# A hybrid encoder block on one core: eleven units of the output projection read their moving columns from 2, 4, 8 or 16 pieces

## The chip, the cores and the metric

The kernel runs on one core of a Trainium2 chip. The metric is the device time of one execution in microseconds (us). Two runs of the kernel before gave 907.03 and 907.22 us, median 907.12 us. The profiled execution took 907.02 us, of which the span from its first to its last instruction is 905.3 us. PE is TensorE's matmul side, PEld its loading of the stationary operand, DVE is VectorE, ACT is ScalarE, POOL is GpSimd, SP is the engine that issues most of the loads.

## The reference, cut to what matters

One encoder block over 256 tokens of width 2048, all in float32. What touches the change is the output projection, which multiplies the 2048 concatenated group outputs of each token by a 2048 x 2048 matrix:

```python
h = _rmsnorm(x, norm1_g)
proj = h @ w_in
...
a = _rmsnorm(_window_attention(q, k, v, sink), attn_out_g)
f = _rmsnorm(_fourier_mix(u, w_fourier), fourier_out_g)
x = x + jnp.concatenate([a, f], axis=-1) @ w_out
x = x + _conv_ffn(_rmsnorm(x, norm2_g), w_up, dw_w, dw_b, w_down)
return _rmsnorm(x, normf_g)
```

## The kernel before, in words

Weights stream through the core in units of 128 x 2048 float32 (1 MB). For each unit, `load` (line 172) has SP fetch it into a buffer `raw` (three buffers), and `split` (line 179) makes two float32r tiles of it: ACT copies it, rounded, into `hi` (line 185), and DVE writes the rest, `raw - hi`, into `lo` (line 186). Both lie in one tile `parts` (three buffers) of 4224 elements a partition. `parts_tile` (line 167) sets where: for a unit of kind "moving", as the output projection's are, `hi` starts at element 0 and `lo` at element 2048. A product of two float32 matrices then takes three float32r matmuls: hi x hi, lo x hi, hi x lo.

The work runs in a written order, one unit after another: `unit` (line 415) does the unit's matmuls, and `step` (line 395) then splits the unit two places ahead. Units 0 to 3 of the plan belong to the Fourier input, 4 to 7 to the values, 8 to 23 to keys and queries (`N_OUT` is 24), 24 to 39 to the output projection, and the rest to the feed-forward part. Other work (attention steps, sums, transposes) is hung before, beside or behind a unit by `at`.

A unit of the output projection (the loop from line 831 on) holds the weights of one block of 512 output columns `c` and one quarter `kq` of the 2048 inputs: four tiles q of 128 inputs x 512 columns. `OUT_ORDER` (line 54) lists (c, kq). For each of the two halves b of the tokens, `moving_weights` (line 365) runs over the four tiles. The stationary operand is a 128 x 128 block of `cat` (inputs x tokens) and the moving operand is the tile of weights, in three matmuls (lines 370 to 372) of 512 columns each:

```python
for q, k in enumerate(kk, q0):
    ah, al = (block(act(k), part, b, halves) for part in range(2))
    wh, wl = (in_turn(w[:, q * n : (q + 1) * n]) for w in (hi, lo))
    nc.tensor.matmul(ps, ah, wh, start=first and q == q0, stop=False)
    nc.tensor.matmul(ps, al, wh, start=False, stop=False)
    nc.tensor.matmul(
        ps, ah, wl, start=False, stop=last and q == q0 + len(kk) - 1
    )
```

So a unit is 2 x 4 x 3 = 24 matmuls of 512 columns. The results are accumulated in PSUM in `ps_a` (attention inputs, kq 0 to 2) or `ps_ff` (Fourier inputs, kq 3).

The moving columns of a tile are not read one after another. `in_turn` (line 130) reads the 512 elements of a tile from two pieces of 256, one element of the first, one of the second, and so on; the pieces lie 256 elements (1 KB) apart. The host has permuted the weights so that the columns come out in their order. Every float32r matmul of this kernel reads its moving operand from two pieces 1 KB apart: `from_halves` (line 136) does it for attention, `still_weights` (line 376, lines 387 and 389) for the matmuls whose stationary operand is the weights.

Of the kernel before, what the change touches and what calls it, by code (L numbers as in the profile page):

```python
# [9 lines left out]
F32R = mybir.dt.float32r  # L10
# [3 lines left out]
P = 128  # L14
# [37 lines left out]
N_OUT = N_QK + len(QK_ORDER)  # L52

OUT_ORDER = [(0, 0), (1, 0), (0, 1), (1, 1), (0, 3), (0, 2), (1, 3), (1, 2)]
OUT_ORDER += [(c, k) for c in (2, 3) for k in range(4)]


GROUPS = [list(range(4))] + [list(range(k, k + 8)) for k in range(4, 36, 8)]
# [38 lines left out]
def block_kernel(  # L97
# [22 lines left out]
    wp = ctx.enter_context(tc.tile_pool(name="wp", bufs=1))  # L120
# [9 lines left out]
    def in_turn(ap):  # L130
        return ap.rearrange("p (a e) -> p e a", a=2)
# [30 lines left out]
    raws, halves = {}, {}  # L162
# [4 lines left out]
    def parts_tile(name, place):  # L167
        t = wp.tile([P, 2 * 2048 + 128], F32R, tag="parts", name=name, bufs=3)
        oh, ol = PLACES[place]
        return t[:, oh : oh + 2048], t[:, 2048 + ol : 4096 + ol]  # L170
# [8 lines left out]
    def split(i):  # L179
        if i >= len(units):  # L180
            return
        _, n, place = units[i]
        raw = raws[i][:, 0:n]
        hi, lo = (t[:, 0:n] for t in parts_tile(f"parts{i}", place))
        nc.scalar.activation(hi, raw, AF.Copy)  # L185
        nc.vector.tensor_tensor(lo, raw, f32(hi), ALU.subtract)  # L186
        halves[i] = hi, lo
        load(i + RAW)
        load_more(i + RAW)
# [32 lines left out]
    ps = bank(dn, "ps_warm")  # L222
# [19 lines left out]
    for c in range(4):  # L242
        t = base.tile([P, 4, 512], F32R, tag=f"hT{c}", name=f"hT{c}")
# [42 lines left out]
    k = 0  # L286
# [75 lines left out]
        nc.vector.tensor_copy(by_parity(dst), ps.rearrange("p (a e) -> p a e", a=2))  # L362


    def moving_weights(hi, lo, n, kk, act, b, ps, first, last, q0=0, halves=False):

        for q, k in enumerate(kk, q0):
            ah, al = (block(act(k), part, b, halves) for part in range(2))
            wh, wl = (in_turn(w[:, q * n : (q + 1) * n]) for w in (hi, lo))
            nc.tensor.matmul(ps, ah, wh, start=first and q == q0, stop=False)  # L370
            nc.tensor.matmul(ps, al, wh, start=False, stop=False)  # L371
            nc.tensor.matmul(  # L372
                ps, ah, wl, start=False, stop=last and q == q0 + len(kk) - 1
            )
# [456 lines left out]
    for n, (c, kq) in enumerate(OUT_ORDER):  # L831
        i = N_OUT + n

        def work(hi, lo):
            if kq == 0:
                ps_a[c] = [bank(mm, f"ps_a{c}{b}") for b in range(2)]
            if kq == 3:
                ps_a[c, "f"] = [bank(dn, f"ps_ff{c}{b}") for b in range(2)]
            ps = ps_a[c] if kq < 3 else ps_a[c, "f"]
            for b in range(2):  # L840
                moving_weights(
                    hi, lo, 512, range(4 * kq, 4 * kq + 4), cat.get, b, ps[b],
                    kq in (0, 3), kq in (2, 3),
                )

        unit(i, work)
        if kq >= 2:
            part = "a" if kq == 2 else "f"
            ps = ps_a[c] if kq < 3 else ps_a[c, "f"]
            last = c in added  # L850
            added.add(c)
            if n == len(OUT_ORDER) - 1:
                later.append(out_post(c, part, ps))
                continue

            at(behind if (c, kq) == (0, 2) else beside, i + 1, out_add, c, part, ps)
            if last:
                at(behind, i + 1, out_sums, c)
                at(before, i + 2, lambda c=c: st.update({("x", c): turn_x_in(c)}))
                at(beside, i + 2, lambda c=c: turn_x_out(c, st.pop(("x", c))))  # L860
# [7 lines left out]
    parts = {}  # L868
    gate_out, sums_of, act = {}, {}, {}
# [288 lines left out]
    for q in range(2):  # L1158
        kind, j = items[q]
        ps = bank(mm, f"ps_{kind}{j}")  # L1160
# [16 lines left out]
    for n, it in enumerate(items):  # L1177
# [8 lines left out]
        if it[0] in ("gate", "val"):  # L1186
            kind, j = it
            ps = bank(mm, f"ps_{kind}{j}")
# [4 lines left out]
        if it[0] == "product":  # L1193
            kind, g, c, p = it
            hi, lo = halves.pop(it)
            both = c == 2
            shape = (2, 1024) if both else (4, 512)
            for cc in (0, 1) if both else (c,):
                o = 512 * cc if both else 0
                if (cc, p) in held:  # L1200
                    first, end = (g, c) == FIRST_SET[cc], (g, c) == LAST_SET[cc]
                    by_parts(held[cc, p], parts[p], hi, lo, first, end, *shape, o)
                    continue
                ps = bank(mm, f"ps_{p}{g}{cc}")
# [6 lines left out]
        else:  # L1211
            kind, g, c = it
            hi, lo = halves.pop(up_index[n])
            ps = [bank(mm, f"ps_l{g}{c}{b}") for b in range(2)]
# [10 lines left out]
    i = up_index[n]  # L1225
# [49 lines left out]
def _layout(inp):  # L1275

    import numpy as np

    f = lambda a: np.ascontiguousarray(np.asarray(a), dtype=np.float32)
    x = f(inp["x"]).reshape(P, 2, D)  # L1280
    by_parity = np.arange(S).reshape(P, 2).T.reshape(-1)

    def in_turn(w):

        return f(w).reshape(*w.shape[:-1], -1, 256, 2).swapaxes(-1, -2).reshape(w.shape)

    def tiles(v):
        return f(v).reshape(-1, P).T

    def moving(w, cols):  # L1290

        return in_turn(w[:, cols]).reshape(-1, 4, P, cols.stop - cols.start).transpose(
            0, 2, 1, 3
        ).reshape(-1, P, 4 * (cols.stop - cols.start))

    def still(w, c0):

        return f(w[:, c0 : c0 + P]).reshape(-1, P, P).transpose(1, 0, 2).reshape(1, P, -1)

    w_in = np.asarray(inp["w_in"])  # L1300
    start = {"q": 0, "k": AW}
    kv = NKV * HD
    win = np.concatenate(
        [moving(w_in, slice(AW + kv, AW + 2 * kv))]
        + [still(w_in, start[t] + h * HD) for t, h in QK_ORDER]
    )
    u0 = AW + 2 * kv
    u_rows = np.concatenate(
        [x.transpose(1, 0, 2).reshape(S, NK, P).transpose(2, 1, 0),
         in_turn(w_in[:, u0 : u0 + FW]).reshape(NK, P, FW).transpose(1, 0, 2)], axis=2,  # L1310
    )
    w_out = np.asarray(inp["w_out"])
    wout = np.concatenate(
        [moving(w_out, slice(c * 512, (c + 1) * 512))[k : k + 1] for c, k in OUT_ORDER]
    )
    w_up = np.asarray(inp["w_up"])
    wup = np.concatenate(
        [still(w_up, o + j * P) for j in range(NF) for o in (0, DFF)]
    )
    w_dn = np.asarray(inp["w_down"])  # L1320
    def rows_by(tiles, cols, width=512):

        w = in_turn(w_dn[tiles[0] * P : (tiles[-1] + 1) * P, cols : cols + width])
        return w.reshape(len(tiles), P, width).transpose(1, 0, 2).reshape(P, -1)

    downs = []
    for g, c in SETS:
        half = len(GROUPS[g]) // 2
        width = 1024 if c == 2 else 512
        for k in (GROUPS[g][0], GROUPS[g][half]):  # L1330
            for n in (0, 1024):
                downs.append(rows_by(range(k, k + half), n + (0 if c == 2 else 512 * c), width))
    late = [rows_by(LATE, 512 * c) for c in range(4)]
    dw = f(inp["dw_w"]).reshape(3, NF, P).transpose(2, 1, 0).reshape(P, 3 * NF)
    sink = np.broadcast_to(f(inp["sink"])[None, :], (P, NH))
    vecs = np.concatenate(
        [tiles(inp["norm1_g"]), tiles(inp["norm2_g"]), tiles(inp["attn_out_g"]),
         tiles(inp["fourier_out_g"]), dw, tiles(inp["dw_b"]), sink], axis=1,
    )
    t = np.arange(S)  # L1340
    ang = 2.0 * np.pi * ((t[:, None] * t[None, :]) % S) / S
    c_pos = np.concatenate(
        [np.cos(ang[:, : S // 2 + 1]), np.sin(ang[:, 1 : S // 2])], axis=1
    )
    c_pos = c_pos[by_parity].reshape(2, P, P, 2).transpose(1, 3, 0, 2)
    k = np.arange(P)
    ang = 2.0 * np.pi * ((k[:, None] * k[None, :]) % P) / P
    c_chan = np.concatenate([np.cos(ang), -np.sin(ang)], axis=1) / np.sqrt(S * P)
    dist = np.abs(t[:, None] - t[None, :]).astype(np.float64)
    c_rel = np.where(dist <= WINDOW, dist, FAR)[by_parity][:, by_parity]  # L1350
    c_rel = c_rel.reshape(2, P, S).transpose(1, 0, 2)
    return {
        "x": x,
        "u_in": np.concatenate([tiles(inp["norm1_g"]), u_rows.reshape(P, -1)], axis=1),
        "vecs": np.ascontiguousarray(vecs),
        "wf": in_turn(f(inp["w_fourier"]).transpose(1, 0, 2).reshape(P, FW)),
        "w_in": win,
        "w_out": wout,
        "w_up": wup,
        "w_down": np.stack(downs),  # L1360
        "w_down_late": np.stack(late),
        "w_down_last": np.stack([rows_by(LAST, 512 * c) for c in range(4)]),
        "normf_g": f(inp["normf_g"]),
        "c_pos": np.ascontiguousarray(c_pos.reshape(P, 2 * S), dtype=np.float32),
        "c_chan": np.ascontiguousarray(c_chan, dtype=np.float32),
        "c_rel": np.ascontiguousarray(c_rel.reshape(P, 2 * S), dtype=np.float32),
    }
# [16 lines left out]
```

## Time and profile before

| | before |
|---|---|
| median of two runs | 907.12 us |
| profiled execution | 907.02 us |
| its span | 905.3 us |
| PE busy | 896.0 us (99%) |
| DVE busy | 746.2 us (82%) |
| ACT busy | 547.0 us (60%) |
| DMA moved | 214.86 MB, mean 237 GB/s |
| the output projection's matmuls | 384 of 512 columns, from 155.1 to 245.1 us |

A share of busy time is a mean over the span. Matmuls overlap in the pipeline: the profile's duration of one (380 ns for 512 columns) reaches from its start to its modelled end, and the next one starts before that. What a matmul costs in time is the distance from its start to the start of the next, which the timeline and the chain of work show. A group's row has its line, engine, operation and tiles, its shapes and count, then its busy time and mean ns of one, then the idle time of the engine before it and what ended that.

### The profile page before, as it was taken

What the parts mean: (1) busy time and instruction counts of PE and PEld (TensorE: products, weight loads), DVE (VectorE), ACT (ScalarE), POOL (GpSimd) and SP (SyncE); (2) the same over time, 40 slices, a digit from 0 to 9 for tenths busy, and PEclk for the clock granted to TensorE, in tenths of its full rate; (3) what the DMA queues carried; (4) which work ended last, traced back from release to release, by engine and by line L of the source; (5) the groups of instructions that cost most, each with busy time, mean ns of one, the idle gap of its engine ahead of it and who ended that gap; (6) DMA issues with size and microseconds to landing.
All of it is one profiled execution on the core that took longest, in us unless ns stands there. A gap on an engine that the chain in (4) does not pass through costs nothing.

```text
span 905.3 us, 12755 instructions
## 1 busy us (share of the span) xinstructions
PE 896.0 (99%) x5075; PEld 812.7 (90%) x5075; DVE 746.2 (82%) x893; ACT 547.0 (60%) x662; POOL 50.2 (6%) x64
## 2 busy tenths in 40 slices
PE   9999999999999999999999999999999999999996
PEld 8899999888899999999999999999999999999885
DVE  7579888666668877889887998878988789998996
ACT  7757677555554656556565565566655566656644
POOL 0001111000000000000000000000000000000003
PEclk9999999999999999999999999999999999999999
DMA  9864544456568677677898779887887988779652
GB/s 359 337 227 152 186 150 177 143 184 222 197 239 275 231 239 254 186 255 234 273 261 277 244 257 286 262 275 236 275 250 245 317 257 268 241 238 293 210 192 93
DMA packets 32764, 214.86 MB, mean 237 GB/s; under 512 B 3616, under 2 KB 3872, under 8 KB 8384
## 3 DMA queue, kind: packets, MB, share of 16 engines
q1 hardware_dynamic: 28592, 184.55, 54.5%
q0 software_dynamic: 4112, 29.49, 17.4%
q8 instruction: 40, 0.66, 0.3%
q14 instruction: 20, 0.16, 0.0%
HBM read 211.93 MB, written 2.10 MB: 236 GB/s over the span
## 4 chain that ended last, share of the span: by engine, by line
PE 95%; DVE 3%; POOL 1%; issue 1%; ACT 0%; ACTq 0%; POOLq 0%; DVEq 0%
PE ps_val L387 17%; PE ps_gate L387 17%; PE ps_val L389 8%; PE ps_gate L389 8%; PE ps_q L387 5%; PE ps_P L1098 3%; PE ps_P L1100 3%; PE ps_P L1099 3%; PE ps_N L1098 2%; PE ps_N L1099 2%; PE ps_N L1100 2%; PE ps_u L281 2%; PE ps_q L389 2%; PE ps_a L370 2%; PE ps_a L371 2%; PE ps_a L372 2%
## 5 line engine op out<-in xcount | busy, mean ns | idle before, releaser
L186 DVE TENSOR_TENSOR parts<-raw,parts 128x2048 fp32r<-128x2048 f32 (+1 forms) x129 | 293.2, 2273 | 48.7 <-ACT parts L185 47.9
L185 ACT ACTIVATE parts<-raw 128x2048 fp32r<-128x2048 f32 (+1 forms) x129 | 245.5, 1903 | 46.0 <-PE ps_a L372 12.4
L387 PE MATMUL ps_val<-hU,parts 128*128 128x512 f32 x688 | 227.7, 382 | 0.0
L387 PE MATMUL ps_gate<-hU,parts 128*128 128x512 f32 x688 | 227.3, 382 | 0.0
L389 PE MATMUL ps_val<-hU,parts 128*128 128x256 f32 x688 | 187.7, 273 | 0.0
L389 PE MATMUL ps_gate<-hU,parts 128*128 128x256 f32 x688 | 187.0, 273 | 0.0
L387 PEld LDWEIGHTS ps_val<-hU,parts 128*128 128x128 f32 x688 | 130.2, 189 | 18.0
L387 PEld LDWEIGHTS ps_gate<-hU,parts 128*128 128x128 f32 x688 | 130.1, 189 | 18.0
L389 PEld LDWEIGHTS ps_val<-hU,parts 128*128 128x128 f32 x688 | 132.3, 192 | 0.7
L389 PEld LDWEIGHTS ps_gate<-hU,parts 128*128 128x128 f32 x688 | 132.1, 192 | 0.9
L876 ACT ACTIVATE ft_g<-ps_gate 128x256 f32<-128x256 f32 x43 | 16.5, 383 | 112.6 <-PE ps_gate L389 110.0
L387 PE MATMUL ps_q<-hT,parts 128*128 128x512 f32 x192 | 62.6, 384 | 0.0
L876 ACT ACTIVATE ft_v<-ps_val 128x256 f32<-128x256 f32 x43 | 16.4, 382 | 73.4 <-PE ps_val L389 73.4
L1098 PE MATMUL ps_P<-parts_P,op_P 128*128 128x512 f32 x144 | 54.7, 380 | 0.0
L1100 PE MATMUL ps_P<-parts_P,op_P 128*128 128x512 f32 x144 | 54.7, 380 | 0.0
L1099 PE MATMUL ps_P<-parts_P,op_P 128*128 128x512 f32 x144 | 54.7, 380 | 0.0
L389 PE MATMUL ps_q<-hT,parts 128*128 128x256 f32 x192 | 50.4, 273 | 0.0
L984 DVE TENSOR_TENSOR parts_N<-sumw,parts_N 128x2048 fp32r<-128x2048 f32 x18 | 41.2, 2288 | 10.0 <-ACT parts_N L983 9.9
L1098 PE MATMUL ps_N<-parts_N,op_N 128*128 128x512 f32 x108 | 41.0, 380 | 0.0
L1100 PE MATMUL ps_N<-parts_N,op_N 128*128 128x512 f32 x108 | 41.0, 380 | 0.0
L1099 PE MATMUL ps_N<-parts_N,op_N 128*128 128x512 f32 x108 | 41.0, 380 | 0.0
L387 PEld LDWEIGHTS ps_q<-hT,parts 128*128 128x128 f32 x192 | 36.1, 189 | 4.6
(344 smaller groups left out, 1558.9 us busy)
## 6 DMA issues: line engine op xcount, KB each, us to landing
raw<-in_w_up SPq DMA_DIRECT2D x86, 1024.0 KB, 6.0
raw<-in_w_in SPq DMA_DIRECT2D x20, 1024.0 KB, 4.9
sumw<-in_w_down POOLq DMA_DIRECT2D x18, 1024.0 KB, 8.7
raw<-in_w_out SPq DMA_DIRECT2D x16, 1024.0 KB, 4.8
raw<-in_w_down_late SPq DMA_DIRECT2D x4, 1024.0 KB, 5.9
u_raw<-in_u_in SPq DMA_DIRECT2D x4, 768.0 KB, 10.8
raw<-in_w_down_last SPq DMA_DIRECT2D x4, 768.0 KB, 4.6
u_raw<-in_u_in SPq DMA_DIRECT2D x7, 384.0 KB, 6.5
```

The source lines that it names most:

```text
L185: nc.scalar.activation(hi, raw, AF.Copy)
L186: nc.vector.tensor_tensor(lo, raw, f32(hi), ALU.subtract)
L281: nc.tensor.matmul(ps_u[b], block(hk(k), part, b, True), in_turn(w), start=k == 0 and n == 0, stop=k == NK - 1 and n == 2,)
L370: nc.tensor.matmul(ps, ah, wh, start=first and q == q0, stop=False)
L371: nc.tensor.matmul(ps, al, wh, start=False, stop=False)
L387: nc.tensor.matmul(ps, hi[:, s], in_turn(h), start=k == 0, stop=False)
L389: nc.tensor.matmul(ps[:, 0:S], lo[:, s], in_turn(h)[:, 0:P], start=False, stop=k == NK - 1)
L876: nc.scalar.activation(tmp, ps[:, S : 2 * S], AF.Copy)
L984: nc.vector.tensor_tensor(lo, src, f32(hi), ALU.subtract)
L1098: nc.tensor.matmul(ps, o[:, 0, p, :], wh, start=first and p == 0, stop=False)
L1099: nc.tensor.matmul(ps, o[:, 1, p, :], wh, start=False, stop=False)
L1100: nc.tensor.matmul(ps, o[:, 0, p, :], wl, start=False, stop=end)
```

## The change

For eleven of the sixteen units of the output projection, numbers 1 to 7 and 9 to 12, the four tiles of 512 columns are laid out in another way in the unit's 2048 elements, and the matmuls read them in turn from another number of pieces at another distance. Units 0, 8, 13, 14 and 15 stay as they were. The table `READS` gives the number of pieces, their distance in elements of 4 bytes, the start of each of the four tiles, and a gap:

| unit | pieces | distance | elements a piece | c, kq |
|---|---|---|---|---|
| 1 | 4 | 512 B | 128 | 1, 0 |
| 2 | 2 | 2 KB | 256 | 0, 1 |
| 3 | 4 | 1 KB | 128 | 1, 1 |
| 4 | 8 | 1 KB | 64 | 0, 3 |
| 5 | 2 | 4 KB | 256 | 0, 2 |
| 6 | 8 | 256 B | 64 | 1, 3 |
| 7 | 4 | 2 KB | 128 | 1, 2 |
| 9 | 16 | 128 B | 32 | 2, 1 |
| 10 | 16 | 512 B | 32 | 2, 2 |
| 11 | 2 | 4 KB + 16 B | 256 | 2, 3 |
| 12 | 2 | 4 KB + 64 B | 256 | 3, 0 |

For units 11 and 12, `split` writes `hi` and `lo` in two rows of 1024 elements with the gap (4 or 16 elements) between them, so that the two pieces are 1028 or 1040 elements apart. `columns` builds the view that a matmul reads, and the host places the weights to match. The number of matmuls, their columns, their stationary operands, their order and the loads are the same.

```diff
+READS = {
+    1: (4, 128, [0, 512, 1024, 1536], 0),
+    2: (2, 512, [0, 256, 1024, 1280], 0),
+    3: (4, 256, [0, 128, 1024, 1152], 0),
+    4: (8, 256, [0, 64, 128, 192], 0),
+    5: (2, 1024, [0, 256, 512, 768], 0),
+    6: (8, 64, [0, 512, 1024, 1536], 0),
+    7: (4, 512, [0, 128, 256, 384], 0),
+    9: (16, 32, [0, 512, 1024, 1536], 0),
+    10: (16, 128, [0, 32, 64, 96], 0),
+    11: (2, 1024, [0, 256, 512, 768], 4),
+    12: (2, 1024, [0, 256, 512, 768], 16),
+}
...
         hi, lo = (t[:, 0:n] for t in parts_tile(f"parts{i}", place))
+        gap = READS.get(i - N_OUT, (0, 0, 0, 0))[3]
+        if gap:
+            t = wp.tile([P, 2 * 2048 + 128], F32R, tag="parts", name=f"parts{i}", bufs=3)
+            hi, lo = (
+                t[:, o : o + 2 * (1024 + gap)].rearrange("p (a e) -> p a e", a=2)[:, :, 0:1024]
+                for o in (0, 2 * (1024 + gap))
+            )
+            raw = raw.rearrange("p (a e) -> p a e", a=2)
         nc.scalar.activation(hi, raw, AF.Copy)
         nc.vector.tensor_tensor(lo, raw, f32(hi), ALU.subtract)
...
+    def columns(w, n, q, reads):
+        if reads is None:
+            return in_turn(w[:, q * n : (q + 1) * n])
+        pieces, far, places, gap = reads
+        o, m = places[q], n // pieces
+        if gap:
+            return w[:, :, o : o + m].rearrange("p a e -> p e a")
+        across = 2048 // (pieces * far)
+        w = w.rearrange("p (z a d) -> p z d a", z=across, a=pieces)
+        z, o = divmod(o, pieces * far)
+        return w[:, z, o : o + m, :]
+
-    def moving_weights(hi, lo, n, kk, act, b, ps, first, last, q0=0, halves=False):
+    def moving_weights(
+        hi, lo, n, kk, act, b, ps, first, last, q0=0, halves=False, reads=None
+    ):
 
         for q, k in enumerate(kk, q0):
             ah, al = (block(act(k), part, b, halves) for part in range(2))
-            wh, wl = (in_turn(w[:, q * n : (q + 1) * n]) for w in (hi, lo))
+            wh, wl = (columns(w, n, q, reads) for w in (hi, lo))
...
                 moving_weights(
                     hi, lo, 512, range(4 * kq, 4 * kq + 4), cat.get, b, ps[b],
-                    kq in (0, 3), kq in (2, 3),
+                    kq in (0, 3), kq in (2, 3), reads=READS.get(i - N_OUT),
                 )
```

The rest of the diff is on the host: `by_pieces` puts every `pieces`-th column of a tile into one piece.

More of the change, by code (lines that the diff above doesn't have):

```diff
@@ L1312, in _layout, with by_pieces @@
     w_out = np.asarray(inp["w_out"])
+    def by_pieces(n, w):
+        if n not in READS:
+            return in_turn(w).transpose(1, 0, 2).reshape(1, P, 2048)
+        pieces, far, places, _ = READS[n]
+        out = np.zeros((1, P, 2048), np.float32)
+        for o, tile in zip(places, w):
+            for a in range(pieces):
+                at = o + a * far
+                out[0, :, at : at + 512 // pieces] = tile[:, a::pieces]
+        return out
     wout = np.concatenate(
-        [moving(w_out, slice(c * 512, (c + 1) * 512))[k : k + 1] for c, k in OUT_ORDER]
+        [by_pieces(n, f(w_out[k * 512 : (k + 1) * 512, c * 512 : (c + 1) * 512]).reshape(
+            4, P, 512)) for n, (c, k) in enumerate(OUT_ORDER)]
     )
```

## The prediction

> **What bounds the kernel now.** I read the page first: busy shares, the 40 slices, the chain of work that ended last.
>
> ```profile
> span 905.3 us, 12755 instructions
> PE 896.0 (99%) x5075; PEld 812.7 (90%) x5075; DVE 746.2 (82%) x893; ACT 547.0 (60%) x662; POOL 50.2 (6%) x64
> ...
> PEclk9999999999999999999999999999999999999999
> ...
> PE 95%; DVE 3%; POOL 1%; issue 1%; ACT 0%; ACTq 0%; POOLq 0%; DVEq 0%
> ```
>
> PE is busy 99% of the span, its granted clock never drops, and 95% of the chain is PE. So the kernel is bound by TensorE as a whole. The change sits in one stage, so next come a window over that stage, its groups by line, and its waits.
>
> ```profile
> 155.10:245.10 90.00, 90.00 (x450) 1.00 0.54 187
> ```
>
> ```profile
> L370 PE MATMUL ps_a<-parts,cat 128*128 128x512 f32 x96 | 36.9, 384 | 0.0
> L186 DVE TENSOR_TENSOR parts<-raw,parts 128x2048 fp32r<-128x2048 f32 x16 | 36.7, 2291 | 12.5 <-ACT parts L185 12.2
> L371 PE MATMUL ps_a<-parts,cat 128*128 128x512 f32 x96 | 36.4, 380 | 0.0
> L372 PE MATMUL ps_a<-parts,cat 128*128 128x512 f32 x96 | 36.4, 380 | 0.0
> L185 ACT ACTIVATE parts<-raw 128x2048 fp32r<-128x2048 f32 x17 | 32.5, 1912 | 21.5 <-PE ps_a L372 12.4 <-PE ps_ff L372 9.1
> ...
> L370 PE MATMUL ps_ff<-parts,cat 128*128 128x512 f32 x32 | 12.2, 382 | 0.0
> L372 PE MATMUL ps_ff<-parts,cat 128*128 128x512 f32 x32 | 12.1, 380 | 0.0
> L371 PE MATMUL ps_ff<-parts,cat 128*128 128x512 f32 x32 | 12.1, 380 | 0.0
> ```
>
> In the stage of the output projection, from 155.1 to 245.1 us, PE is busy 90.00 of 90.00 us at a clock of 1.00, and its matmuls have no idle time before them. ACT is the one that waits: 21.5 us for PE to be done with a `parts` buffer. So each nanosecond that a matmul of this stage gains or loses goes into the end of the kernel, and nothing hides it.
>
> The duration of 380 ns is not the price of a matmul, since the next starts sooner. The price is the distance between starts. Here are two rows of the timeline, 20 matmuls apart, from unit 1 of the stage:
>
> ```profile
> 162.00 0.38 PE L370 MATMUL ps_a<-parts,cat 128*128 128x512 f32 x1
> ...
> 166.32 0.38 PE L372 MATMUL ps_a<-parts,cat 128*128 128x512 f32 x1
> ```
>
> 20 distances in 4.32 us are 216 ns for 512 columns, 0.42 ns a column. A unit of 24 matmuls takes 24 x 216 ns = 5.18 us, and the eleven changed units hold 264 matmuls, 57.0 us.
>
> **The change part by part.** *The reads.* The count of matmuls, their columns, stationary operands and order stay. What changes is the order of addresses from which the moving columns come. Before, two pieces 1 KB apart supply them; afterwards there are 2, 4, 8 or 16 pieces, at 128 B to 4 KB. The trace holds no such read, so its price has to be bounded.
>
> The lower bound comes from the fixed part of a matmul. Two rows of the chain of work give other reads on the same engine:
>
> ```profile
> 166.70 0.67 PE ps_o L727 x6
> 167.36 0.44 PE ps_t L705 x4
> ```
>
> Six matmuls of 256 columns (also from two pieces 1 KB apart) in 0.67 us are 112 ns each. Twice that is 224 ns for 512 columns, against 216 ns for one matmul of 512, so at most 8 ns of a matmul does not grow with its columns. If another order of addresses removed all of that, 264 x 8 ns = 2.1 us would be gained; the columns themselves go through at 0.42 ns each, at the full granted clock, and an order of reading does not change their number. The lower end is -2.1 us.
>
> The upper bound comes from the second row. Four transposes of 128 columns in 0.44 us are 110 ns each, 0.86 ns a column, twice the price of a column above. They are the reads in this stage that go straight through a block instead of from two pieces in turn. They are plain float32 in transpose mode, so their price may come from the mode and not from the addresses. As an upper end it serves: a read at that price makes 512 columns cost 440 ns, 224 ns more, 24 x 224 ns = 5.4 us a unit, and 264 x 224 ns = 59 us for all eleven.
>
> Between these ends, the nearest rows are those of the same read with the same number of columns at another place in memory: the feed-forward matmuls read 512 and 256 columns in turn, from two pieces 1 KB apart, out of the activations instead of the weights. The timeline:
>
> ```profile
> 599.88 0.38 PE L387 MATMUL ps_gate<-hU,parts 128*128 128x512 f32 x1
> ...
> 602.83 0.38 PE L387 MATMUL ps_gate<-hU,parts 128*128 128x512 f32 x1
> ```
>
> Nine pairs in 2.95 us are 327.8 ns for 768 columns. At the 216 ns for 512 columns of the output projection they would be 324.0. So with other tiles at other places the same columns cost 1.2% more, 2.5 ns on 512 columns. Part of this can be the second matmul's fixed price. I take this 2.5 ns for each of the 264 matmuls: 264 x 2.5 ns = 0.7 us. I take it because these rows are float32r matmuls with the same alternating read, whereas the transposes differ in type, mode and columns. The reads before already leave one address for another 1 KB away at each single element, 512 times a matmul, and run at 0.42 ns a column; a read that jumps to a third and a fourth piece makes no more jumps than that.
>
> [...]
>
> *The gap units 11 and 12.* ACT and DVE write `hi` and `lo` in two rows of 1024 instead of one of 2048. At 1912 and 2291 ns a unit (rows above) they are 4.2 us in sequence, against 5.18 us of PE, and two units ahead of use. The second row costs at most another start of an instruction; both engines' own idle time in the stage, 21.5 and 12.5 us, covers it. Without that cover, 1 us a unit would be missing before PE waited. Cost: 0.
>
> *The loads.* SP fetches the same 1 MB for each unit into the same buffers; only the host's arrangement differs. Cost: 0. If PE became slower, the `parts` buffers would come free later, ACT would wait longer than 21.5 us, and the loads behind would start later by the same time; everything after moves with PE, and nothing is given back, since PE is the one that waits for nothing.
>
> **The sum.** Reads +0.7 us, gap units 0, loads 0. The profiled execution took 907.02 us (its span of 905.3 and 1.7 us around it), 0.1 us under the median of 907.12. From the median: 907.8 us.
>
> **The rivals.**
>
> *Slower, because only two places are kept open.* If the reader of the moving operand keeps up with two pieces but not with four, each column of the seven units with 4, 8 or 16 pieces (1, 3, 4, 6, 7, 9, 10) costs the 0.86 ns of the transposes: 7 x 5.4 us = 38 us, 945 us. For it: every read in the trace at 0.42 ns a column comes from two pieces, and the only others run at 0.86. Against it: the type of those others explains them as well. It decides from a mean of 18.1 us / 264 = 69 ns more on each of the matmuls, a third of their 216.
>
> *Slower, by the distance.* If two successive elements must lie in different parts of the memory, and 1 KB is a distance at which they do, then 2 KB and 4 KB may not be: units 2, 5, 7, 11 and 12, 5 x 5.4 us = 27 us, 934 us. The short distances (units 6 and 9, 256 and 128 B) alone would give 11 us, 918 us. For it: the trace has no distance but 1 KB. Against it: the hU and the weights lie at quite different addresses and differ by 2.5 ns.
>
> *A small price.* Ten to 69 ns on the mean matmul, because some patterns meet the loading of the stationary operand, or the writes of ACT and DVE, in the same part of the memory: 909.7 to 925.3 us. For it: PEld is busy 90% of the span, so each moving read runs beside a stationary one, and the 2.5 ns above shows that places do matter a little.
>
> *Faster, or the change does nothing.* The lower end, 2.1 us less, gives 905.0 us; at exactly 216 ns it is 907.1. Both are within 2%.
>
> **How the numbers follow.** All eleven patterns within 10 ns of 216 (up to 264 x 10 ns = 2.6 us): 0.50, my forecast. A small price, or the short distances alone: 0.25. Two places kept open: 0.12. By the distance at 2 and 4 KB: 0.08. A gain of up to 2.1 us: 0.05. Two per cent is 18.1 us, about what a measurement of this kernel can tell from no change: slower by more takes one of the two large cases, 0.20; faster by more is beyond the lower end, 0.01; within is the rest, 0.79. The forecast's own range is 906.4 to 909.7. The range that leaves out no more than 0.2 has to take in the small prices up to 926.0; below, the gain by the lower end is mostly left out, since no row shows a matmul of 512 columns faster than 216 ns: 906.4.
>
> **What would show it.** The timeline of each changed unit: starts 216 to 226 ns apart if the forecast is right, with units 0, 8, 13, 14 and 15 as a measure in the same run. Starts 300 to 440 ns apart in all units of four pieces or more, and 216 in units 2, 5, 11 and 12, would be the first rival; slow units at 2 and 4 KB whatever the pieces, the second; a rise that grows with the pieces and stays under 100 ns, the third. ACT's wait for `ps_a` in the stage (21.5 us with `ps_ff`) grows by what PE loses. The forecast is wrong if the mean distance in the changed units is over 285 ns, or if the time moves without those distances.

## The result, and the profile after

The changed kernel takes 938.03 us (937.96 to 938.09, two runs) against 907.12 us, a ratio of 1.0341 with a 95% interval of 1.0325 to 1.0358: slower by 31 us. The forecast was 907.8 us, with a range up to 926.0.

The page of the kernel after, in the lines that answer to those of before:

```profile
span 936.3 us, 12755 instructions
PE 926.8 (99%) x5075; PEld 813.8 (87%) x5075; DVE 746.8 (80%) x893; ACT 547.3 (58%) x662; POOL 50.4 (5%) x64
...
PEclk9999999999999999999999999999999999999999
```

The same 12755 instructions, the same clock, and DVE and ACT busy for the same time as before within 0.6 us. PE is busy longer by 30.8 us, nearly all that the span grew (31.0 us); PEld, which runs beside it, by 1.1 us. The stage of the output projection in two rows of the windows view, before and after (stretch, PE busy, PEld, DVE, ACT, POOL):

```profile
155.10:245.20 90.10, 90.10 (x451) 79.61 (x450) 61.25 (x74) 46.66 (x62) 3.91 (x5) 1.00 0.54 187
```

```profile
155.60:276.20 120.60, 120.60 (x451) 81.58 (x450) 61.67 (x75) 47.00 (x62) 3.91 (x5) 1.00 0.40 140
```

The stage grew from 90.1 to 120.6 us with the same 451 matmuls, and PE is without a gap in both. ACT, which waited 21.5 us for PE to free a `parts` buffer before, now waits 26.9 + 15.6 = 42.5 us:

```profile
ACT parts L208 <- PE ps_a L409: 26.9, 6, 10.8
...
ACT parts L208 <- PE ps_ff L409: 15.6, 3, 9.1
```

That is 21.0 us more, where the prediction had this wait grow by all that PE loses. The other 9.6 us are in ACT's waits for other results of PE in the stage: `ps_x` (4.2 to 10.8 us), `ps_t` (7.1 to 8.5) and `ps_o` (2.8 to 4.4).

Where in the stage it went, the timeline shows. Each pair of rows below spans 20 matmuls of one unit, as in the prediction, in the order of units 2, 3, 4, 9 and 10:

```profile
170.27 0.38 PE L407 MATMUL ps_a<-parts,cat 128*128 128x512 f32 x1
...
174.58 0.38 PE L409 MATMUL ps_a<-parts,cat 128*128 128x512 f32 x1
...
176.75 0.45 PE L407 MATMUL ps_a<-parts,cat 128*128 128x512 f32 x1
...
182.41 0.45 PE L409 MATMUL ps_a<-parts,cat 128*128 128x512 f32 x1
...
184.85 0.67 PE L407 MATMUL ps_ff<-parts,cat 128*128 128x512 f32 x1
...
194.59 0.67 PE L409 MATMUL ps_ff<-parts,cat 128*128 128x512 f32 x1
...
227.47 0.62 PE L407 MATMUL ps_a<-parts,cat 128*128 128x512 f32 x1
...
236.17 0.63 PE L409 MATMUL ps_a<-parts,cat 128*128 128x512 f32 x1
...
238.19 0.74 PE L407 MATMUL ps_a<-parts,cat 128*128 128x512 f32 x1
...
248.85 0.73 PE L409 MATMUL ps_a<-parts,cat 128*128 128x512 f32 x1
```

They give 216, 283, 487, 435 and 533 ns a matmul. Worked out in the same way for all units:

| unit | pieces, distance | ns a matmul | over 216 ns, x 24 |
|---|---|---|---|
| 2, 5, 11, 12 | 2, at 2 KB, 4 KB, 4 KB + 16 B, 4 KB + 64 B | 216 | 0 |
| 1 | 4 at 512 B | 273 | 1.4 us |
| 3, 7 | 4 at 1 KB, at 2 KB | 283 | 1.6 us each |
| 4, 6 | 8 at 1 KB, at 256 B | 487 | 6.5 us each |
| 9 | 16 at 128 B | 435 | 5.3 us |
| 10 | 16 at 512 B | 533 | 7.6 us |
| 0, 8, 13 to 15 | as before | 216 | 0 |

The last column sums to 30.5 us, the growth of the stage. So the loss of the stage lies in the reads of seven units. In this run it goes roughly by the number of pieces, though sixteen at 128 B cost less than eight; no distance costs anything with two pieces.

### The profile page after: what moved, and what is told of

Same layout as the page of the kernel before. It is cut to its first block, busy times and chain, and to the rows that moved or that the text cites. A ratio compares the mean times of both kernels' runs of the same rounds, so it can differ in the third digit from the quotient of the medians.

```text
span 936.3 us, 12755 instructions
## 1 busy us (share of the span) xinstructions
PE 926.8 (99%) x5075; PEld 813.8 (87%) x5075; DVE 746.8 (80%) x893; ACT 547.3 (58%) x662; POOL 50.4 (5%) x64
## 4 chain that ended last, share of the span: by engine, by line
PE 91%; DMA 3%; DVE 3%; issue 1%; POOL 1%; ACT 1%; SPq 1%; ACTq 0%; POOLq 0%; DVEq 0%
PE ps_val L424 16%; PE ps_gate L424 16%; PE ps_gate L426 8%; PE ps_val L426 8%; PE ps_q L424 4%; PE ps_P L1135 3%; PE ps_P L1137 3%; PE ps_P L1136 3%; PE ps_a L408 3%; PE ps_a L409 3%; PE ps_a L407 3%; PE ps_N L1135 2%; PE ps_N L1137 2%; PE ps_N L1136 2%; PE ps_q L426 2%; DMA raw<-in_w_in 2%
## 5 line engine op out<-in xcount | busy, mean ns | idle before, releaser
L208 ACT ACTIVATE parts<-raw 128x2048 fp32r<-128x2048 f32 (+1 forms) x129 | 245.6, 1904 | 67.8 <-PE ps_a L409 26.9
L407 PE MATMUL ps_a<-parts,cat 128*128 128x512 f32 x96 | 43.2, 450 | 0.0
L408 PE MATMUL ps_a<-parts,cat 128*128 128x512 f32 x96 | 42.8, 446 | 0.0
L409 PE MATMUL ps_a<-parts,cat 128*128 128x512 f32 x96 | 42.8, 446 | 0.0
L1135 PE MATMUL ps_N<-parts_N,op_N 128*128 128x512 f32 x108 | 41.0, 380 | 0.0
```

What stands on the lines that cost most here:

```text
L409: nc.tensor.matmul(ps, ah, wl, start=False, stop=last and q == q0 + len(kk) - 1)
L1135: nc.tensor.matmul(ps, o[:, 0, p, :], wh, start=first and p == 0, stop=False)
```

## The experiments

The question left was what a piece costs. Three theories stood at first, guesses of mine all three. L: the number of pieces decides; a reader of the moving operand is supposed to keep a few lines of 16 bytes, and a line fetched for a single column to cost two columns' time (sixteen pieces at 128 B took 435 ns, against 216). B: pieces conflict by their distance, which was always a multiple of 128 bytes where there were more than two. C: the loops of the address pattern cost, whatever the addresses.

A line here and below is four neighbouring elements that begin at a multiple of 16 bytes from the start of `parts`. No view shows a reader or what it keeps. That these groups of four matter is shown by two runs further down: four successive elements from each of sixteen pieces in turn took 283 ns for 512 columns, and 505 when shifted by 8 bytes; groups of four at jumps of 64 bytes, from two pieces in turn, took 216 ns, and 251 and 232 when shifted by 4 and by 8 bytes.

For all experiments `columns` takes the moving operand's pattern itself from the table, and the host places the weights to match (in part, against the changed kernel):

```diff
-        pieces, far, places, gap = reads
...
+        dims, starts, _, _, _ = reads
+        return bass.AP(w.tensor, w.offset + starts[q], [list(w.ap[0])] + [list(d) for d in dims])
```

An entry of the table is: the pattern (step in elements and count, outermost first), the starts of the four tiles, the rows of a tile and the gap between them, and a shift of both tiles, all in elements of 4 bytes. Of the tables below only some entries are shown. The runs with many patterns were executed once each; in every one of them the unchanged units 0 and 8 stand at 216 ns, so the distances between starts can be compared from run to run.

### Two pieces alone

```diff
+    2: ([(1, 256), (512, 2)], [0, 256, 1024, 1280], 1, 0, 0),
+    5: ([(1, 256), (1024, 2)], [0, 256, 512, 768], 1, 0, 0),
+    11: ([(1, 256), (1028, 2)], [0, 256, 512, 768], 2, 4, 0),
+    12: ([(1, 256), (1040, 2)], [0, 256, 512, 768], 2, 16, 0),
```

> Only the four units with two pieces are changed (2, 5, 11 and 12: distances 2 KB, 4 KB, 4 KB + 16 B, 4 KB + 64 B); the seven with four or more pieces are as in the kernel before. Theory L (the reader of the moving operand keeps few lines of 16 bytes, so the number of pieces decides): 216 ns a matmul in all units, 907.1 us, within 0.3 us of the kernel before. Theory B (the distance decides, by parts of the memory that the pieces share): 216 ns here as well, since the changed kernel had it there; so this run only tests that the loss lies in the other seven units. If it comes out over 908 us, part of the 31 us has another source than the reads.

907.07 us, ratio to the kernel before 0.9999 (0.999 to 1.0009). The four units with two pieces, the rows with gaps among them, cost nothing.

### Other distances, and one piece

```diff
+    1: ([(1, 128), (260, 4)], [0, 128, 1040, 1168], 8, 4, 0),
...
+    4: ([(1, 64), (260, 8)], [0, 64, 128, 192], 8, 4, 0),
...
+    7: ([(8, 64), (1, 4), (4, 2)], [0, 512, 1024, 1536], 1, 0, 0),
...
+    12: ([(1, 512)], [0, 512, 1024, 1536], 1, 0, 0),
...
```

> The changed kernel's distances with four and more pieces were all multiples of 128 bytes. Here the same numbers of pieces are read at other distances: unit 1 four at 1 KB + 16 B, 2 four at 1 KB + 32 B, 3 four at 2 KB + 64 B, 4 eight at 1 KB + 16 B, 5 eight at 1 KB + 32 B, 6 sixteen at 512 + 16 B; then neighbouring lines: 7 two at 16 B, 9 four at 16 B, 10 eight at 16 B, 11 sixteen at 16 B; 12 one piece straight through; 13 four at 64 B, 14 eight at 64 B; 15 four at 1 KB with both tiles shifted by 64 B. Theory L (a few lines of 16 bytes are kept; number of pieces decides, distance does not): 283 ns a matmul for four, 487 for eight, 435 to 532 for sixteen at every distance, 216 for two and for one, in all about 957 us. Theory B (pieces conflict when their distance is a multiple of 128 B or another power of two): 216 ns in units 1 to 6 and 9 to 11, only 13, 14 and 15 slow, about 917 us. Theory C (the steps of the address pattern cost, whatever the addresses): by the length of the innermost loop, 283 for four, 487 for eight and about 480 for sixteen, as L. If shifting the tiles changes unit 15 from 283, the place against the stationary operand matters.

The whole took 949.09 us. Unit 4 (eight pieces at 1 KB + 16 B) and unit 12 (one piece) in the timeline, 20 matmuls a pair:

```profile
184.89 0.61 PE L416 MATMUL ps_ff<-parts,cat 128*128 128x512 f32 x1
...
193.65 0.61 PE L418 MATMUL ps_ff<-parts,cat 128*128 128x512 f32 x1
...
257.84 0.39 PE L416 MATMUL ps_a<-parts,cat 128*128 128x512 f32 x1
...
262.38 0.40 PE L418 MATMUL ps_a<-parts,cat 128*128 128x512 f32 x1
```

438 ns with eight pieces at a distance that is no multiple of 128 bytes, and 227 ns straight through one piece. The others: four pieces 268 to 280 ns, eight 433 to 480, sixteen 461, two at 16 B 216. Theory B falls: no distance brings four or more pieces back to 216 ns. Distance has a second, smaller part (433 to 487 ns for eight). L and C stand, but L had 216 ns for one piece, 11 ns too little. The shift by 64 B of unit 15 changed 283 ns to 280.

### Runs and steps

```diff
+    1: ([(2, 64), (256, 4), (1, 2)], [0, 128, 1024, 1152], 1, 0, 0),
...
+    6: ([(4, 16), (256, 8), (1, 4)], [0, 64, 128, 192], 1, 0, 0),
...
+    12: ([(1, 2), (2, 256)], [0, 512, 1024, 1536], 1, 0, 0),
...
```

> Runs and steps. Units 2, 3 and 5 leave out 8, 8 and 128 of their 512 columns; their price goes by the column. Unit 1: four pieces at 1 KB, two successive elements from each; 4: eight at 1 KB, two from each; 6: eight at 1 KB, four from each (a whole line); 7: sixteen at 512 B, two from each; 9: sixteen, four from each; 10: the same with the tiles shifted by 8 B, so that each run of four covers halves of two lines; 2: six pieces, 3: twelve pieces, 5: six at 1 KB; 11: eight at 1 KB as in the changed kernel, beside other neighbours; 12, 13, 14: one piece with steps of 8, 16 and 32 B; 15: sixteen at 128 B as in the changed kernel. Theory L (the price is that of fetching a line of 16 bytes, about 0.85 ns, twice a column's 0.42; a line read by two successive elements or more goes at full rate): 216 ns in units 1, 4, 6, 7, 9, 10 and 12 whatever the pieces; 430 to 435 in 13 and 14, where each element lies in a line of its own and nothing is returned to; 487 in 11, 435 in 15; six pieces between four and eight (0.55 to 0.95 ns a column); in all about 942 us. Theory B (conflict by distance): runs of two take half the loss only (350 ns for eight pieces, 370 for sixteen), and 13 and 14 are 216 since neighbouring lines do not conflict. Theory C (the address pattern's loops): 13 and 14 are 216, their inner loop being long; 4, 6, 7, 9 and 10, with three loops, are as slow as with two or slower, 435 ns and more.

The whole took 972.57 us, without the columns that units 2, 3 and 5 leave out. Unit 1 (four pieces, two elements from each) and unit 12 (one piece, steps of 8 bytes):

```profile
162.57 0.62 PE L416 MATMUL ps_a<-parts,cat 128*128 128x512 f32 x1
...
171.43 0.62 PE L418 MATMUL ps_a<-parts,cat 128*128 128x512 f32 x1
...
268.43 0.64 PE L416 MATMUL ps_a<-parts,cat 128*128 128x512 f32 x1
...
277.46 0.64 PE L418 MATMUL ps_a<-parts,cat 128*128 128x512 f32 x1
```

443 and 452 ns, where L had 216 for both. Two successive elements from each of four pieces are worse than one (283 ns). Two from each of eight or sixteen pieces helped nothing (487, 532), four did (280 and 283), and four shifted by 8 bytes did not (505). Through one piece with steps of 16 and 32 bytes (units 13 and 14) it was 461 and 431 ns. Six pieces took 291 ns for 504 columns and 235 for 384, twelve 427 for 504, and sixteen at 128 B again 435. L is wrong as it stood. So is C: unit 1 here has the loops of 64, 4 and 2 that unit 7 of the run before had, 443 ns against 216, and units 13 and 14 miss the 216 that C, and B too, had for them.

All of this falls into order if the addresses of the even and of the odd columns of a matmul are taken as two lists. Theory M: what counts is how many columns of one list lie in a line, and among how many lines that list goes in turn. The expectations below call the lists an even and an odd reader; that is a name, and no view shows how the columns are fetched. With two pieces in turn, the even list is piece one and the odd list piece two, each straight through, four columns to a line (216 ns). With one piece, each list takes every second element, two to a line (227). With one piece and steps of 8 bytes each list makes steps of 16 bytes, one to a line (452). With two elements from each of four pieces, each list has four lines in turn (443).

### The even and the odd columns as two lists

```diff
+    1: ([(16, 64), (1, 4), (1024, 2)], [0, 4, 8, 12], 1, 0, 0),
...
+    3: ([(4, 256), (1024, 2)], [0, 1, 2, 3], 1, 0, 0),
+    4: ([(2, 128), (1024, 2), (1, 2)], [0, 256, 512, 768], 1, 0, 0),
...
+    12: ([(2, 256), (1024, 2)], [0, 1, 512, 513], 1, 0, 0),
...
```

> Two pieces 4 KB apart, one element from each in turn, except where stated. Unit 1: each piece is read by whole lines of 16 bytes (four elements) at jumps of 64 bytes; 2: by half lines (two elements) at jumps of 32 bytes; 3: by single elements 16 bytes apart; 12: by single elements 8 bytes apart; 9 and 10: as unit 1 with the tiles shifted by 4 and by 8 bytes, so that each four lie in two lines, 3 + 1 or 2 + 2. Units 4, 5, 6: two pieces, but two, four, eight successive elements from each in turn. Unit 13: four pieces 2 KB apart, four from each. Unit 7: ten pieces (2 of 512 columns left out). Unit 11: one piece, shifted by 64 bytes. Units 14 and 15: four pieces at 1 KB and at 1 KB + 16 B, shifted by 16 and 64 bytes. Theory M (an even and an odd reader; what counts is how many columns of its own a reader finds in a line, or in the two or three lines it keeps): unit 1 216 ns; 2, 10 and 12 two to a line, between 227 (one piece) and 284; 9 between 216 and 284; 3 one to a line, 430 to 461; 4 two lines in turn, 270 to 284; 5, 6 and 13 two to a line, 227 to 284; 7 about 430; 11 227; 14 and 15 270 to 284. Theory S (each reader needs steps of 4 bytes): 12 as slow as one piece with steps of 8 bytes was, 451 ns; 2, 9, 10 and 1 slowed by their jumps. Theory L1 (one reader that keeps two or three lines): 4, 5, 6, 2 and 12 216 ns; it has already missed one piece with steps of 8 bytes (216 expected, 451 measured).

The whole took 930.1 us. Units 1, 3, 4 and 12, 20 matmuls a pair:

```profile
161.58 0.38 PE L416 MATMUL ps_a<-parts,cat 128*128 128x512 f32 x1
...
165.90 0.38 PE L418 MATMUL ps_a<-parts,cat 128*128 128x512 f32 x1
...
175.22 0.64 PE L416 MATMUL ps_a<-parts,cat 128*128 128x512 f32 x1
...
184.25 0.63 PE L418 MATMUL ps_a<-parts,cat 128*128 128x512 f32 x1
...
186.39 0.51 PE L416 MATMUL ps_ff<-parts,cat 128*128 128x512 f32 x1
...
193.19 0.51 PE L418 MATMUL ps_ff<-parts,cat 128*128 128x512 f32 x1
...
243.03 0.40 PE L416 MATMUL ps_a<-parts,cat 128*128 128x512 f32 x1
...
247.60 0.39 PE L418 MATMUL ps_a<-parts,cat 128*128 128x512 f32 x1
```

216, 452, 340 and 228 ns. The last is the clearest: elements 8 bytes apart cost 452 ns from one piece and 228 from two in turn, with as many columns to a line in both; what differs is that a second piece supplies the odd columns. Theory S (451) and L1 (216) miss it. Unit 1 jumps 64 bytes after each line and takes the 216 ns of the reads before, where S had it slowed. Two to a line by a shift of 8 bytes (unit 10) took 232 ns, 3 + 1 by 4 bytes (unit 9) 251, half lines (unit 2) 232; four and eight successive elements from each piece (units 5 and 6) 250 and 243, four from each of four (13) 267. As M had them came one piece shifted by 64 bytes (unit 11, 229) and four pieces at 1 KB and 1 KB + 16 B with a shift (units 14 and 15, 273 and 271). Misses of M: unit 4, 340 ns where I had 270 to 284, and ten pieces, 520 for 510 columns where I had 430. In unit 4 each list goes to and fro between two lines and finds two of its columns in each; in four pieces one element at a time (273 ns) it also goes between two, but finds four in each. So the number of lines in turn and the columns in each both count.

### One piece in all sixteen units

```diff
+    0: ([(1, 512)], [0, 512, 1024, 1536], 1, 0, 0),
...
+    15: ([(1, 512)], [0, 512, 1024, 1536], 1, 0, 0),
```

> All sixteen units of the output projection read their 512 columns from one piece, straight through, which the run with gaps had at 227 ns a matmul in one unit. Theory M (two readers, one for the even and one for the odd columns; each goes at full rate where a line of 16 bytes gives it four successive columns, and pays where it gives fewer): 227 ns in all units, 16 x 24 x 11 ns = 4.2 us, 911.2 us. Theory S (each reader needs successive steps of 4 bytes): steps of 8 bytes in both readers, so 227 too. If 227 ns was due to the neighbours of that one unit, the units differ here.

911.25 us, ratio 1.0047 (1.003 to 1.0063): 227 to 228 ns in units 3 and 9 by the timeline, and the stage took 94.5 us (154.9 to 249.4) against 90.1, a mean of 11 ns more on its 384 matmuls. Reading in turn from two pieces is worth 4.3 us in this stage.

### The prices used to foretell new reads

```diff
+    1: ([(2, 128), (512, 4)], [0, 1, 256, 257], 1, 0, 0),
+    2: ([(4, 128), (512, 4)], [0, 1, 2, 3], 1, 0, 0),
...
+    5: ([(32, 64), (1, 4), (4, 2)], [0, 8, 16, 24], 1, 0, 0),
...
```

> Theory M with the prices measured so far, by how many lines a reader has in turn and how many of its columns it finds in each: one line, four columns 216 ns; one, two 227 to 250; one, one 431 to 461; two, four 268 to 283; two, two 340; four, four or fewer 433 to 487. New reads: unit 1, four pieces at 2 KB with steps of 8 bytes (two lines, two columns): 340; 9, the same at 2 KB + 64 B: 320 to 340; 2, four pieces with steps of 16 bytes (two, one): 431 to 487; 3 and 10, two pieces, two elements from each in turn, at 4 KB + 64 B and at 1 KB (two, two): 340; 4, four pieces by whole lines at jumps of 64 B (two, four): 268 to 283; 5, 64 pieces at 128 B of two lines in turn (one, four): 216; 11, the same without jumps: 216; 6, 64 pieces at 128 B, eight elements straight through (one, two): 227 to 250; 7, eight pieces at 1 KB with steps of 8 bytes (four, two): 433 to 487. If instead the number of pieces decides, 1, 2, 4 and 9 are alike at 270 to 284, and 5, 6 and 11 over 435.

Units 1, 2 and 5:

```profile
162.27 0.50 PE L412 MATMUL ps_a<-parts,cat 128*128 128x512 f32 x1
...
168.93 0.52 PE L414 MATMUL ps_a<-parts,cat 128*128 128x512 f32 x1
...
171.80 0.69 PE L412 MATMUL ps_a<-parts,cat 128*128 128x512 f32 x1
...
181.46 0.69 PE L414 MATMUL ps_a<-parts,cat 128*128 128x512 f32 x1
...
198.78 0.38 PE L412 MATMUL ps_a<-parts,cat 128*128 128x512 f32 x1
...
203.10 0.38 PE L414 MATMUL ps_a<-parts,cat 128*128 128x512 f32 x1
```

333, 483 and 216 ns. The rest: unit 3 329, unit 4 269, unit 6 232, unit 7 443, unit 9 327, unit 10 333, unit 11 216. Units 1, 3 and 10 lie 2 to 3% under the 340 that I gave, the others within what I gave. The kernel took 931.42 us.

### Sixty-four pieces at full rate

All eleven units with the pattern of unit 5 above:

```diff
+    1: ([(32, 64), (1, 4), (4, 2)], [0, 8, 16, 24], 1, 0, 0),
...
+    12: ([(32, 64), (1, 4), (4, 2)], [0, 8, 16, 24], 1, 0, 0),
```

> All eleven changed units read each tile from 64 pieces, 128 bytes apart: from each piece eight elements, those of two neighbouring lines of 16 bytes in turn, so that of the even columns four successive ones lie in one line and of the odd columns four in the other. Theory M (an even and an odd reader, each at full rate with four columns of its own to a line): 216 ns a matmul, 907.0 us, within 0.4 us of the kernel before. If it is the number of pieces or of jumps that costs, 64 pieces are slower than the sixteen at 128 bytes were (435 ns), 965 us or more.

Unit 1, the unit of the pair in the prediction:

```profile
162.00 0.38 PE L413 MATMUL ps_a<-parts,cat 128*128 128x512 f32 x1
...
166.32 0.38 PE L415 MATMUL ps_a<-parts,cat 128*128 128x512 f32 x1
```

907.09 us, ratio 1.0 (0.9991 to 1.001), and 216 ns in units 1 and 9 by the timeline. With 64 pieces a tile nothing is lost where each list finds four of its columns in a line before it leaves it. Neither the number of pieces nor that of jumps is the cause by itself.

## Why the prediction was wrong

- *What bounds the stage.* Right. PE had no gap before and has none after, and every nanosecond of the reads came out at the end: 30.5 us in the units, 31.0 us in the span. The other 0.5 us lies ahead of the stage, which began at 155.7 instead of 155.1 us; in runs with the same work ahead it began between 154.6 and 155.1 us.
- *Two pieces at other distances, the gap units, the loads.* Right: 216 ns, and the run with these four units alone is at 907.07 us. In the changed kernel `split` takes 1.91 and 2.02 us on ACT and 2.29 us on DVE for the two units with two rows; over the stage the means are 1.92 and 2.29. The second rival (conflict by distance) is out: at 2 and 4 KB nothing is lost, and eight pieces cost 487 ns at 256 B as at 1 KB.
- *The price of the reads with four pieces and more.* This is the step that failed. I took 2.5 ns a matmul, from the feed-forward rows. Those rows were float32r and read in turn, but from two pieces like all others: they held the very thing fixed that the change altered, so they were no nearest row for it. Nor were the 2.5 ns a price of other places: the prediction's own rows, 216 ns for 512 columns and 112 for 256, add up to 328 for a pair, and 327.8 was what the pair took. Measured were 57 to 317 ns on a matmul of the seven units; the mean distance over all eleven is 331 ns, above the 285 that the prediction named as the sign of its being wrong. The sentence behind it, that a read leaves its address at each element already and more pieces make no more jumps, was wrong in its count. The reads before do jump at each column, but from the even columns to the odd ones; taken by themselves, the even columns go straight through one piece and the odd ones through the other. With four pieces each of the two lists goes to and fro between two, with eight it goes round four, and with sixteen round eight.
- *The upper end.* 224 ns more was near the truth for sixteen pieces at 128 B (219) and short of it for eight (271) and for sixteen at 512 B (317). A single column to a line, with nothing returned to, costs 431 to 461 ns for 512 columns, the 440 taken from the transposes; going to and fro between lines can cost more. That the 440 from the transposes came so near to this is luck. The 110 ns of a transpose of 128 columns need not be 0.86 ns a column: in the same stage of the kernel before, four plain float32 matmuls of a single column each take 85 ns apiece, so most of the price of such short matmuls may not grow with the columns.

```profile
190.30 0.34 PE ps_tota L496 x4
```

And a float32r read straight through one piece, which is the order of the transposes, takes 227 ns. So that order does not make the 440, and what does in the transposes is not shown.

- *The lower end.* No read came under 216 ns.
- *The first rival* (only two places kept open, chance 0.12) had the units and the direction right, and 945 us against 938.03. Its price was wrong for four pieces: 1.4 to 1.6 us a unit, not 5.4. That is 11.5 us too much in three units, against 4.4 us too little in the other four, so the nearness of the sum is partly luck. Its mechanism was not quite it either: 64 pieces run at 216 ns.
- *The third rival* put the extra price on collisions with the stationary reads or with the writes of ACT and DVE. Eight pieces at 1 KB gave 487 ns in the changed kernel's unit 4 and again in unit 11 of the run with runs and steps, beside other neighbours; one piece gave 227 to 228 ns in units 3 and 9 and a mean of 11 ns more over all sixteen units, and the pattern of 64 pieces 216 in units 1 and 9 and 907.09 us with all eleven, with other work beside them each time. That speaks against it as the main part. What part it has in the differences by distance is open.

Counted over all columns, the number of columns to a line does not order the prices: one piece with steps of 8 bytes has two to each line and takes 452 ns, two pieces in turn with elements 8 bytes apart have two as well and take 228. Counted for the even and the odd columns apart, where no line is returned to, it comes nearer: one to a line costs 431 to 505 ns, two 227 to 283, four 216. A list that goes to and fro between two lines, leaving each after a single column, still takes only 268 to 283 where it comes back for four.

The two lists are a way to sort the prices; no view shows how the columns are read. What is shown is that the reads with up to three lines in turn are sorted by them, with one exception (505 ns), and not by pieces, distances, loops or lines over all columns. From four lines on the prices lie between 427 and 533 ns, in no order that the lists give.

## What to carry to other kernels

For a float32r matmul like these (512 moving columns), write down the addresses of the even columns and of the odd columns separately, and lay the moving operand out so that each of the two lists takes whole 16-byte lines, four elements one after the other: then 512 columns took 216 ns here, with the next line up to 128 bytes further on, against 227 straight through one piece and 427 to 533 where each list finds one element in a line or goes round four lines and more. When a change alters one property of an access, look whether any row of the trace differs in just that property; if none does, the rows that are otherwise alike say nothing of its price, and the upper bound deserves its weight.

## What the runs showed of the hardware that was not expected

Prices of 512 columns, by what the list of the even or of the odd columns meets, over all runs:

| lines in turn | columns of its own in each line | ns for 512 columns |
|---|---|---|
| 1 | 4 | 216 |
| 1 | 2 | 227 to 250; 267, 280 and 283 with four, eight and sixteen pieces far apart |
| 1 | 3 and 1 by turns | 251 |
| 1 | 1 | 431 to 461; 505 with sixteen pieces far apart |
| 2 | 4 | 268 to 283 |
| 2 | 2 | 327 to 340 |
| 2 | 1 | 483 |
| 3 | 4 | 291 for 504 columns, 235 for 384 |
| 4 | 4 or 2 | 433 to 487 |
| 5, 6 | 4 | 520 for 510 columns, 427 for 504 |
| 8 | 4 or 2 | 435 to 533 |
| 16 | 2 | 532 |

So three lines in turn took little longer than two (291 ns for 504 columns, against 268 to 283 for 512), and from four on it was 427 to 533 ns, about twice the 216 of one line; five lines took longer than six (520 and 427). Inside a row the distance moves the price by about a fifth (sixteen pieces: 435 ns at 128 B, 461 at 16 B and at 528 B, 533 at 512 B), and a shift of both tiles by 16 bytes took four pieces at 1 KB from 283 to 273 ns. No rule for that was found, and it was not followed further.
